# Where the seven-product trick is applied in three SwiGLUs of a one-core trunk: up projections in place of down projections

## The chip, the cores and the metric

The kernel runs on one core of a Trainium2 chip. The metric is the device time of one execution in microseconds; the time before is the median of three runs. One more execution was recorded by the hardware profiler; all views of the profile come from it.

## What is computed

A decoder trunk of two layers over 512 tokens of width 1024, in float32. Each layer adds half a SwiGLU, then a mixer (an mLSTM in the first layer, native sparse attention in the second), then half a SwiGLU. There are thus four SwiGLUs, ffn0 to ffn3, with 2816 hidden columns each:

```python
def rmsnorm(x, g):
    return x * lax.rsqrt(jnp.mean(x * x, axis=-1, keepdims=True) + EPS) * g

def swiglu(h, w_in, w_out):
    a, b = jnp.split(h @ w_in, 2, axis=-1)
    return (jax.nn.silu(a) * b) @ w_out

for layer in range(DEPTH):
    h = h + 0.5 * swiglu(rmsnorm(h, ffn_norm[layer, 0]), ffn_w_in[layer, 0], ffn_w_out[layer, 0])
    ...
    h = h + 0.5 * swiglu(rmsnorm(h, ffn_norm[layer, 1]), ffn_w_in[layer, 1], ffn_w_out[layer, 1])
```

The mLSTM's result is normed per head and multiplied by `sigmoid(og)` before its output projection.

## The kernel before

Everything is kept transposed: the stream is eight tiles `h[b]` of 128 features by 512 tokens. A weight block holds eight strips of 128x128. A SwiGLU has 22 blocks `a` (for the silu), 22 blocks `b` and, for the way down, eight output blocks.

**Precision.** Every float32 operand is split into a high and a low part (`split`: ScalarE copies to the high part, VectorE subtracts it for the low one). `mm3` (matmuls on line 215) makes a product of three matmuls, hi x hi, hi x lo and lo x hi. So an up block with 512 tokens is 8 strips x 3 = 24 matmuls of 512 columns, and blocks `a` and `b` together are 48. PSUM takes eight banks of 512 columns.

**Weights.** `weight` hands out weights in the order that a dry run has recorded, and loads two ahead: SP starts the DMA into `wraw` (two buffers), ScalarE makes `whi` and VectorE `wlo` (three buffers each). `plan` puts other steps into the same order.

**Seven products.** Two neighbouring output blocks and two halves of the inner dimension make a 2x2 matrix of weight quarters; the two token halves of 256 columns make the other side 2x2. With sums and differences ("forms") of quarters on both sides, seven products replace eight. In the kernel before this is done in ffn0, ffn1 and ffn3 (`SEVEN`) on the way down: `gate_forms` makes the forms of the gated tiles (`fhi`, `flo`), `fetch` loads four quarters, `add_quarters` makes four sums `s`, `load_forms` splits them in four groups, and `down_seven` runs the seven products of 256 columns into the banks X, Y, Z and V and combines them. The hidden blocks are taken in chunks of 8, 8 and 6 (`EVENS`); of each chunk's four pairs of output blocks, `PAIRS` picks two, two and one for seven products. That makes 15 such pairs in the kernel, twelve with 7 x 4 x 3 = 84 matmuls in place of 48, three with 63 in place of 36. All up blocks, the other down pairs and all of ffn2 are plain.

**Norm.** The up products run on `h` times the gain (`norm_in`: `xhi`, `xlo`). The row factor `r` comes later: `rstd_columns` and `rsqrt`, a chain of eleven small VectorE steps (`rq`, `rc`), then `rstd_rows`, whose matmul `cst,rc` spreads `rc`; the gates multiply by `r`. In ffn0 these are issued in up block 1, at its fourth and thirteenth strip. ffn1 and ffn3 get `r` from the stage before.

**Start.** `setup` loads `h[0]` to `h[7]`, the gains and the first two weights; up block 0 alternates strips of its two halves by a sort key.

**mLSTM.** In `finish` (lines 680 to 760) the numerators `num`, the denominators `ds`, `dc` and the head norm are made; `sigmoids(half)` (line 765) turns `og` into `sig` on ScalarE, and is issued before the `finish` of its half.

The engines run their own queues in order; a scheduler sets the order of one queue's instructions beforehand, from the order and the data needs of the program.

Of the kernel before, what the change touches and what calls it, by code (L numbers as in the profile page):

```python
# [10 lines left out]
F32 = mybir.dt.float32  # L11
# [8 lines left out]
P = 128  # L20
T = 512
# [8 lines left out]

SEVEN = (0, 1, 3)
EVENS = ((0, 8), (8, 16), (16, 22))
PAIRS = {0: (1, 3), 8: (1, 3), 16: (1,)}
# [63 lines left out]
class Net:  # L97
# [64 lines left out]
    def fetch(self, i, m, k0, n):  # L162


        q = {}
        for a in (1, 2):
            for b in (1, 2):
                k = k0 + (b - 1) * n
                t = q[a, b] = self.fp.tile([P, 512], F32, name=f"q{a}{b}", tag=f"q{a}{b}", bufs=1)[:, :n * P]
                ap = self.a["ffn_out"][i, 2 * m + a - 1, slice(None), slice(k, k + n)]  # L170
                self.nc.sync.dma_start(t.rearrange("p (n m) -> p n m", m=P), ap)
        self.raws[i, m, k0] = q

    def add_quarters(self, i, m, k0, n):

        q = self.raws[i, m, k0]
        s = self.sums[i, m, k0] = [None] + [self.fp.tile([P, 512], F32, name=f"s{j}", tag=f"s{j}", bufs=1)[:, :n * P]
                                            for j in range(1, 5)]
        self.nc.vector.tensor_tensor(s[1], q[2, 1], q[2, 2], op=ALU.add)
        self.nc.vector.tensor_tensor(s[3], q[1, 1], q[2, 1], op=ALU.subtract)  # L180
        self.nc.vector.tensor_tensor(s[2], s[1], q[1, 1], op=ALU.subtract)
        self.nc.vector.tensor_tensor(s[4], q[1, 2], s[2], op=ALU.subtract)

    def load_forms(self, i, m, k0, n, group):

        q, s = self.raws[i, m, k0], self.sums[i, m, k0]
        forms = ((q[1, 1], s[2]), (s[1], s[3]), (s[4], q[1, 2]), (q[2, 2],))[group]
        hi = self.wp.tile([P, 1024], F32R, name="whi", tag="whi")
        lo = self.wp.tile([P, 1024], F32R, name="wlo", tag="wlo")
        out = []  # L190
        for j, f in enumerate(forms):
            c = slice(512 * j, 512 * j + n * P)
# [35 lines left out]
    def setup(self):  # L228
# [7 lines left out]
        for b in range(KB):  # L236
# [5 lines left out]
            if b == 1 and self.order:  # L242
                self.load_weight()
# [11 lines left out]
    def norm_in(self, gcol, ssq=True, loaded=False):  # L255
# [82 lines left out]
    def ffn(self, i, r=None):  # L338
# [4 lines left out]
        with ExitStack() as ctx:  # L343
# [8 lines left out]
            def gated(t, pa, pb):  # L352
                u = gp.tile([P, T], F32, name="fu", tag="fu", bufs=2)
                TT(t, pa, r, op=ALU.mult)  # L354
                nc.scalar.activation(t, t, AF.Silu)
                TT(u, pb, r, op=ALU.mult)  # L356
                TT(t, t, u, op=ALU.mult)

            def gate(pa, pb):
                t = gp.tile([P, T], F32, name="ft", tag="ft", bufs=2)  # L360
                gated(t, pa, pb)
# [5 lines left out]
            def gate_forms(pa, pb):  # L367


                fl = lambda t: t.rearrange("p f n -> p (f n)")  # L370
                if not half:
                    t = gp.tile([P, 3 * N], F32, name="ft", tag="ft", bufs=2)
                    gated(t[:, :T], pa, pb)
                    TT(t[:, T:], t[:, :N], t[:, N:T], op=ALU.subtract)
                    hi = gp.tile([P, 8, N], F32R, name="fhi", tag="fhi", bufs=4)
                    lo = gp.tile([P, 8, N], F32R, name="flo", tag="flo", bufs=4)
                    self.split(t, fl(hi[:, :3]), fl(lo[:, :3]))
                    gs.append((hi, lo))
                    half.append(t)
                    return  # L380
                one, (hi, lo) = half.pop(), gs[-1]
                t = gp.tile([P, 5 * N], F32, name="fv", tag="fv", bufs=1)
                gated(t[:, :T], pa, pb)
                self.split(t[:, :T], fl(hi[:, 3:5]), fl(lo[:, 3:5]))
                c = [t[:, N * j:N * j + N] for j in range(5)]
                TT(c[2], c[0], one[:, T:], op=ALU.subtract)
                TT(c[3], c[0], one[:, :N], op=ALU.subtract)
                TT(c[4], c[1], c[2], op=ALU.subtract)  # L388
                self.split(t[:, T:], fl(hi[:, 5:]), fl(lo[:, 5:]))

            def down_plain(m, k0, n):

                w2 = [self.weight("ffn_out", i, 2 * m + j, slice(None), slice(k0, k0 + n)) for j in range(2)]
                if seven and m + 1 in PAIRS[k0]:
                    self.plan("fetch", i, m + 1, k0, n // 2)
                    self.plan("add", i, m + 1, k0, n // 2)
                po = [ps_mm() for _ in range(2)]
                order = [(k, j) for j in range(2) for k in range(n)]
                if m == 0:
                    order.sort(key=lambda o: (o[0] % (n // 2), o[0]) if seven else o)  # L400
                for k, j in order:
                    if seven:
                        f = slice(3 * (k // (n // 2)), 3 * (k // (n // 2)) + 2)
                        g = tuple(t[:, f, :].rearrange("p f n -> p (f n)") for t in gs[k % (n // 2)])
                    else:
                        g = gs[k]
                    first = order.index((k, j)) == min(order.index((q, j)) for q in range(n))
                    last = order.index((k, j)) == max(order.index((q, j)) for q in range(n))
                    self.mm3(po[j], self.strip(w2[j], k), g, first, last)
                    yield  # L410
                for j in range(2):
                    h = self.h[2 * m + j]
                    tail = i == 3 and k0 + n == FB and m == KB // 2 - 1 and j
                    for c in (slice(0, T // 2), slice(T // 2, T)) if tail else (slice(0, T),):
                        STT(h[:, c], po[j][:, c], 0.5, h[:, c], op0=ALU.mult, op1=ALU.add)  # L415

            def down_seven(m, k0, n):

                at = i, m, k0, n

                def product(ps, w, f):
                    for k in range(n):
                        l = w[0][:, k, :], w[1][:, k, :]
                        self.mm3(ps, l, (gs[k][0][:, f, :], gs[k][1][:, f, :]), k == 0, k == n - 1)
                        yield

                h1, h2 = self.h[2 * m], self.h[2 * m + 1]
                X, Y, Z, V = ps_mm(), ps_mm(), ps_mm(), ps_mm()
                two = lambda t: t.rearrange("p (c n) -> p c n", n=N)
                W = gp.tile([P, 3, N], F32, name="fw", tag="fw", bufs=2)  # L430
                u2 = gp.tile([P, N], F32, name="fq", tag="fq", bufs=1)
                q = gp.tile([P, T], F32, name="fr", tag="fr", bufs=1)
                a11, s2 = self.weight("form", *at, 0)
                yield from product(X[:, :N], a11, 1)
                nc.scalar.activation(W[:, 1, :], X[:, :N], AF.Copy)  # L435
                yield from product(X[:, N:], s2, 5)

                TT(u2, X[:, N:], W[:, 1, :], op=ALU.add)
                s1, s3 = self.weight("form", *at, 1)
                yield from product(Y[:, :N], s1, 2)  # L440
                yield from product(Y[:, N:], s3, 6)

                TT(W[:, 0::2, :], u2[:, None, :].to_broadcast([P, 2, N]), two(Y), op=ALU.add)
                TT(q[:, :N], W[:, 2, :], Y[:, :N], op=ALU.add)
                s4, a12 = self.weight("form", *at, 2)
                yield from product(Z[:, :N], s4, 3)
                yield from product(Z[:, N:], a12, 4)

                TT(W[:, :2, :], W[:, :2, :], two(Z), op=ALU.add)
                STT(h1, W[:, :2, :].rearrange("p c n -> p (c n)"), 0.5, h1, op0=ALU.mult, op1=ALU.add)  # L450
                a22 = self.weight("form", *at, 3)[0]
                yield from product(V[:, :N], a22, 7)

                TT(q[:, N:], W[:, 2, :], V[:, :N], op=ALU.add)
                STT(h2, q, 0.5, h2, op0=ALU.mult, op1=ALU.add)

            for k0, k1 in EVENS if seven else THIRDS:
                gs, late, half = [], [], []
                n = k1 - k0
                for p in range(k0, k1):  # L460
                    w2 = self.weight("ffn_in", i, p), self.weight("ffn_in", i, FB + p)
# [863 lines left out]
```

## Time and profile before

| | before |
|---|---|
| median of three runs (lowest, highest) | 2036.55 us (2036.38, 2037.76) |
| the profiled execution | 2037.12 us |
| its span, first to last instruction | 2035.3 us |
| GpSimd busy | 163.7 us (8%) |
| HBM read | 177.10 MB |
| moved by DMA, mean over the span | 92 GB/s |

Lines of the profile name the engine (PE is TensorE's matmuls, PEld its weight loads, DVE VectorE, ACT ScalarE), the line of the kernel and the tiles, result first. "x" is a count. In the groups, busy time and mean duration come first, then the idle time just before and who ended it. Matmuls overlap, so the time that one costs is read from start to start of its neighbours, not from its duration.

### The profile page before, as it was taken

What the parts mean: (1) busy time and instruction counts of PE and PEld (TensorE: products, weight loads), DVE (VectorE), ACT (ScalarE), POOL (GpSimd) and SP (SyncE); (2) the same over time, 40 slices, a digit from 0 to 9 for tenths busy, and PEclk for the clock granted to TensorE, in tenths of its full rate; (3) what the DMA queues carried; (4) which work ended last, traced back from release to release, by engine and by line L of the source; (5) the groups of instructions that cost most, each with busy time, mean ns of one, the idle gap of its engine ahead of it and who ended that gap; (6) DMA issues with size and microseconds to landing.
All of it is one profiled execution on the core that took longest, in us unless ns stands there. A gap on an engine that the chain in (4) does not pass through costs nothing.

```text
span 2035.3 us, 26085 instructions
## 1 busy us (share of the span) xinstructions
PE 2020.1 (99%) x10007; PEld 1677.1 (82%) x10007; DVE 1298.4 (64%) x2192; ACT 885.7 (44%) x1533; POOL 163.7 (8%) x216
## 2 busy tenths in 40 slices
PE   9999999999999999999999999999999999999999
PEld 7888888788778888888888888888777788888887
DVE  7565656767786655657656444445778885565654
ACT  5333334445743333334443322224889863333332
POOL 0000000012200000000101000001444410000000
PEclk9999999999999999999999999999999999999999
DMA  5333322323223333322333333323111123233232
GB/s 189 98 99 94 95 91 68 117 83 94 63 99 103 89 108 94 88 94 88 99 116 115 115 93 93 104 89 102 52 43 43 42 80 102 78 118 94 74 111 80
DMA packets 61084, 188.22 MB, mean 92 GB/s; under 512 B 7328, under 2 KB 9760, under 8 KB 60960
## 3 DMA queue, kind: packets, MB, share of 16 engines
q1 hardware_dynamic: 59568, 183.82, 29.3%
q8 instruction: 78, 1.28, 0.3%
q10 hardware_dynamic: 1008, 1.70, 0.2%
q0 software_dynamic: 384, 1.05, 0.2%
q14 instruction: 46, 0.38, 0.1%
HBM read 177.10 MB, written 2.10 MB: 88 GB/s over the span
## 4 chain that ended last, share of the span: by engine, by line
PE 92%; DVE 3%; ACT 3%; DMA 1%; issue 1%; POOL 0%; SPq 0%; DVEq 0%; ACTq 0%
PE pmm L215 82%; PE S L215 3%; PE po L215 2%; PE vps L215 1%; PE pt L1094 1%; PE paux L215 1%; ACT pr L1062 1%; PE pn L215 1%; DVE wlo L158 1%; ACT whi L157 0%; ACT pth L224 0%; PE pt L215 0%; PE dm L215 0%; DMA q<-in_ffn_out 0%; DMA wraw<-in_ffn_in 0%
## 5 line engine op out<-in xcount | busy, mean ns | idle before, releaser
L215 PE MATMUL pmm<-xhi,whi 128*128 128x512 f32 x1672 | 656.6, 393 | 0.7 <-ACT whi L157 0.5
L215 PE MATMUL pmm<-xhi,wlo 128*128 128x512 f32 x1672 | 652.8, 391 | 0.2
L215 PE MATMUL pmm<-xlo,whi 128*128 128x512 f32 x1672 | 652.3, 390 | 0.6 <-DVE xlo L268 0.6
L157 ACT ACTIVATE whi<-wraw 128x1024 fp32r<-128x1024 f32 (+5 forms) x368 | 329.7, 908 | 640.7 <-PE pmm L215 510.8
L158 DVE TENSOR_TENSOR wlo<-wraw,whi 128x1024 fp32r<-128x1024 f32 (+5 forms) x368 | 386.0, 1057 | 75.2 <-ACT whi L157 73.0
L215 PEld LDWEIGHTS pmm<-xhi,wlo 128*128 128x128 f32 x1672 | 313.4, 187 | 66.7 <-DVE wlo L158 1.1
L215 PEld LDWEIGHTS pmm<-xhi,whi 128*128 128x128 f32 x1672 | 313.7, 188 | 63.6 <-ACT whi L157 1.0
L215 PEld LDWEIGHTS pmm<-xlo,whi 128*128 128x128 f32 x1672 | 313.6, 188 | 62.7 <-DVE xlo L268 1.4
L215 PE MATMUL pmm<-fhi,whi 128*128 128x256 f32 (+1 forms) x699 | 230.9, 330 | 0.0
L215 PE MATMUL pmm<-flo,whi 128*128 128x256 f32 (+1 forms) x699 | 229.0, 329 | 0.0
L215 PE MATMUL pmm<-fhi,wlo 128*128 128x256 f32 (+1 forms) x699 | 228.8, 328 | 0.0
L356 DVE TENSOR_TENSOR fu<-pmm,r 128x512 f32<-128x512 f32 x88 | 60.8, 691 | 252.3 <-PE pmm L215 252.3
L215 PEld LDWEIGHTS pmm<-fhi,whi 128*128 128x128 f32 x699 | 132.7, 190 | 14.8 <-ACT fw L435 2.8
L215 PEld LDWEIGHTS pmm<-flo,whi 128*128 128x128 f32 x699 | 132.7, 190 | 11.9
L215 PEld LDWEIGHTS pmm<-fhi,wlo 128*128 128x128 f32 x699 | 132.6, 190 | 11.8
L415 DVE SCALAR_TENSOR_TENSOR h<-pmm,h 128x512 f32<-128x512 f32 (+1 forms) x67 | 45.5, 682 | 116.4 <-PE pmm L215 116.4
L278 POOL TENSOR_TENSOR ssq<-ssq,sq 128x512 f32<-128x512 f32 x18 | 26.5, 1470 | 1038.2 <-ACT sq L277 1006.0
L1067 POOL TENSOR_SCALAR pr<-pr,rz,gate 128x512 f32<-128x512 f32 (+3 forms) x128 | 81.8, 645 | 108.7 <-DVE rz L1063 92.9
L224 ACT ACTIVATE fhi<-fv 128x512 fp32r<-128x512 f32 x66 | 48.8, 740 | 84.2 <-DVE fv L388 61.0
L1062 ACT ACTIVATE pr<-S,nx,c 128x512 f32<-128x512 f32 (+3 forms) x128 | 78.1, 615 | 6.7 <-PE pt L1094 5.6
L354 DVE TENSOR_TENSOR ft<-pmm,r 128x512 f32<-128x512 f32 x55 | 37.9, 688 | 57.2 <-PE pmm L215 50.9
L224 ACT ACTIVATE whi<-s 128x512 fp32r<-128x512 f32 (+1 forms) x60 | 33.8, 601 | 89.9 <-PE pmm L215 63.7
(341 smaller groups left out, 2762.2 us busy)
## 6 DMA issues: line engine op xcount, KB each, us to landing
wraw<-in_ffn_in SPq DMA_DIRECT2D x175, 512.0 KB, 3.5
wraw<-in_ffn_out SPq DMA_DIRECT2D x32, 512.0 KB, 3.6
q<-in_ffn_out SPq DMA_DIRECT2D x48, 256.0 KB, 2.8
wraw<-in_ffn_out SPq DMA_DIRECT2D x16, 448.0 KB, 3.3
wraw<-in_ffn_out SPq DMA_DIRECT2D x18, 384.0 KB, 3.2
wraw<-in_m_qk SPq DMA_DIRECT2D x8, 512.0 KB, 3.5
wraw<-in_m_v SPq DMA_DIRECT2D x8, 512.0 KB, 3.6
wraw<-in_m_og SPq DMA_DIRECT2D x8, 512.0 KB, 3.5
```

The source lines that it names most:

```text
L157: nc.scalar.activation(hi[:p, c], raw[:p, c], AF.Copy)
L158: nc.vector.tensor_tensor(lo[:p, c], raw[:p, c], hi[:p, c].bitcast(F32), op=ALU.subtract)
L215: self.nc.tensor.matmul(out, lhsT, rhs, start=start, stop=stop)
L224: self.nc.scalar.activation(hi, src, AF.Copy)
L278: (nc.gpsimd if b < 4 else nc.vector).tensor_tensor(t, t, sq, op=ALU.add)
L354: TT(t, pa, r, op=ALU.mult)
L356: TT(u, pb, r, op=ALU.mult)
L415: STT(h[:, c], po[j][:, c], 0.5, h[:, c], op0=ALU.mult, op1=ALU.add)
L1062: nc.scalar.activation(s, S[:, i, :n], AF.Exp, bias=nx[:, i:i + 1], scale=cc, accum_out=z[:, i:i + 1])
L1067: nc.gpsimd.tensor_scalar(s, s, rz[:, i:i + 1], gate[:, tb, gi:gi + 1], op0=ALU.mult, op1=ALU.mult)
L1094: nc.tensor.transpose(pt[:, col:col + P], pr[br][:, ROW[tb] + sb * P:ROW[tb] + sb * P + P], self.ident)
```

## The change

The way down is plain again: `PAIRS`, `gate_forms` and `down_seven` go. In ffn0, ffn1 and ffn3 the up blocks are taken in pairs. The first pair (`p` = 0) stays plain. For each of the ten others the two `a` blocks are plain (2 x 24 matmuls of 512 columns), and the two `b` blocks are made by seven products (84 of 256 columns) instead of 48 of 512: `up_seven`. `fetch` takes quarters of `ffn_in`; `x_forms(k)`, four times per SwiGLU, makes four forms `thi`, `tlo` of 256 columns from `h[k]` and `h[k+4]`. Between the first product into X and the second one, a product into Y is issued.

Two smaller edits: at the start, the second weight is loaded after `h[3]` instead of `h[1]`, the rest of the first one is split one tile later, and the sort key of block 0 puts two more strips of the first half ahead of the second half's first strip. In the mLSTM, `sigmoids(half)` is issued inside `finish`, behind the Square that makes `dc`. Without the seven-product layout, the host no longer permutes `ffn_out`.

```diff
-PAIRS = {0: (1, 3), 8: (1, 3), 16: (1,)}
...
     def fetch(self, *at):
+        i, p = at
...
-                ap = self.a["ffn_out"][i, 2 * m + a - 1, slice(None), slice(k, k + n)]
+                ap = self.a["ffn_in"][i, FB + p + a - 1, slice(None), slice(4 * b - 4, 4 * b)]
...
     def load_forms(self, i, p, group):
-        forms = ((q[1, 1], s[2]), (s[1], s[3]), (s[4], q[1, 2]), (q[2, 2],))[group]
+        forms = ((q[1, 1], s[1]), (s[2], s[3]), (s[4], q[1, 2]), (q[2, 2],))[group]
...
-            if b == 1 and self.order:
+            if b == 3 and self.order:
                 self.load_weight()
...
-            if loaded and b == 1:
+            if loaded and b == 2:
                 self.rest()
...
+            def x_forms(k):
+                g1, g2 = (self.g[:, G_FFN + i * KB + b:G_FFN + i * KB + b + 1] for b in (k, k + 4))
+                one, two = (gp.tile([P, 3 * N], F32, name="fw", tag="fw", bufs=2) for _ in range(2))
+                h2, c = self.h[k + 4], [two[:, N * j:N * j + N] for j in range(3)]
+                nc.scalar.activation(one[:, :T], self.h[k], AF.Copy, scale=g1)
+                TT(one[:, T:], one[:, N:T], one[:, :N], op=ALU.subtract)
+                STT(c[0], h2[:, N:], g2, one[:, T:], op0=ALU.mult, op1=ALU.subtract)
+                STT(c[1], h2[:, N:], g2, one[:, N:T], op0=ALU.mult, op1=ALU.subtract)
+                STT(c[2], h2[:, :N], g2, c[0], op0=ALU.mult, op1=ALU.subtract)
+                hi = gp.tile([P, 4 * N], F32R, name="thi", tag="thi", bufs=4)
+                lo = gp.tile([P, 4 * N], F32R, name="tlo", tag="tlo", bufs=4)
+                self.split(one[:, T:], hi[:, :N], lo[:, :N])
+                self.split(two, hi[:, N:], lo[:, N:])
+                xt.append((hi, lo))
...
+            def up_seven(p):
...
+                a11, s1 = self.weight("form", i, p, 0)
+                yield from product(X[:, :N], a11, 0)
+                nc.scalar.activation(W[:, 0, :], X[:, :N], AF.Copy)
+                yield from product(Y[:, :N], s1, -1)
+                s2, s3 = self.weight("form", i, p, 1)
+                yield from product(X[:, N:], s2, -2)
+                TT(U, X[:, N:], W[:, 0, :], op=ALU.add)
+                yield from product(Y[:, N:], s3, -3)
+                TT(W[:, 1:, :], U[:, None, :].to_broadcast([P, 2, N]), two(Y), op=ALU.add)
+                TT(u2[:, N:], W[:, 2, :], Y[:, :N], op=ALU.add)
+                s4, a12 = self.weight("form", i, p, 2)
+                yield from product(Z[:, N:], s4, 3)
+                yield from product(Z[:, :N], a12, 2)
+                TT(two(u1), W[:, :2, :], two(Z), op=ALU.add)
+                TT(u1, u1, r, op=ALU.mult)
+                a22 = self.weight("form", i, p, 3)[0]
+                yield from product(V[:, :N], a22, -4)
+                TT(u2[:, :N], W[:, 2, :], V[:, :N], op=ALU.add)
+                TT(u2, u2, r, op=ALU.mult)
+                return u1, u2
...
+            def plain(p):
...
                 if p == 0:
-                    order.sort(key=lambda o: o[0] + 1.5 * o[1])
+                    order.sort(key=lambda o: o[0] + 3.5 * o[1])
...
+                    if seven and p == 1 and t >= 12:
+                        x_forms(t - 12)
...
+                    if seven and p:
+                        for j in range(2):
...
+                            if j == 0:
+                                self.plan("fetch", i, p)
+                            w = self.weight("ffn_in", i, p + j)
+                            if j == 0:
+                                self.plan("add", i, p)
+                            pa = ps_mm()
+                            for k in range(KB):
+                                strip(pa, w, k)
+                                yield
+                            ts.append(silu(pa))
+                        us = yield from up_seven(p)
+                        for t, u in zip(ts, us):
+                            gate(t, u)
...
                 nc.scalar.activation(dc, pt[:, :, :H], AF.Square)
+                sigmoids(half)
...
-            sigmoids(0)
             weave(project_v(1), finish(0), 0.25)
...
-            sigmoids(1)
             weave(finish(1), rest, 5)
```

How the order of the queues changes is shown at three places.

First, PE in ffn0, behind the first product of 256 columns into bank X. Before, row by row (line, operation, result<-operands, columns, what the instruction waits for; the number in a wait only names a semaphore):

```order
L215 MATMUL pmm<-fhi,whi 128x256
L215 MATMUL pmm<-flo,whi 128x256
L215 MATMUL pmm<-fhi,wlo 128x256
L215 MATMUL pmm<-fhi,whi 128x256 [waits Activation_49]
L215 MATMUL pmm<-flo,whi 128x256
L215 MATMUL pmm<-fhi,wlo 128x256 [waits DVE_49]
L215 MATMUL pmm<-fhi,whi 128x256
L215 MATMUL pmm<-fhi,whi 128x256 [waits Activation_49]
L215 MATMUL pmm<-flo,whi 128x256
L215 MATMUL pmm<-fhi,wlo 128x256
```

The new order, at the first `up_seven`, from the end of the product into Y on:

```order
L212 MATMUL pmm<-thi,whi 128x256
L212 MATMUL pmm<-tlo,whi 128x256
L212 MATMUL pmm<-thi,wlo 128x256
L212 MATMUL pmm<-thi,whi 128x256 [waits Activation_49]
L212 MATMUL pmm<-tlo,whi 128x256
L212 MATMUL pmm<-thi,wlo 128x256
L212 MATMUL pmm<-thi,whi 128x256 [waits Activation_49]
L212 MATMUL pmm<-tlo,whi 128x256
L212 MATMUL pmm<-thi,wlo 128x256 [waits DVE_49]
L212 MATMUL pmm<-thi,whi 128x256
```

Before, the second product into X begins at the second `waits Activation` (the copy of X's first half), with four matmuls of the product into Y pulled ahead of it. Now it begins at the second `waits Activation` too, but behind the whole of that product: the six rows ahead of it are the last of twelve.

Second, VectorE in up block 1 of ffn0, where the chain `rv`, `rq`, `rc` is worked off. Before:

```order
L158 TENSOR_TENSOR wlo<-wraw,whi 128x1024 [waits DMAHW3_49,Activation_49]
L299 TENSOR_SCALAR rq<-rv 128x4 [waits DVE_49]
L300 TENSOR_SCALAR rc<-rq 128x4 [waits DVE_49]
L302 TENSOR_TENSOR rq<-rc 128x4 [waits DVE_49]
L303 SCALAR_TENSOR_TENSOR rq<-rq,rv 128x4 [waits DVE_49]
L304 SCALAR_TENSOR_TENSOR rc<-rq,rc 128x4 [waits DVE_49]
L302 TENSOR_TENSOR rq<-rc 128x4 [waits DVE_49]
L303 SCALAR_TENSOR_TENSOR rq<-rq,rv 128x4 [waits DVE_49]
L304 SCALAR_TENSOR_TENSOR rc<-rq,rc 128x4 [waits DVE_49]
L302 TENSOR_TENSOR rq<-rc 128x4 [waits DVE_49]
L303 SCALAR_TENSOR_TENSOR rq<-rq,rv 128x4 [waits DVE_49]
```

Now, over the same start of the chain (`fw` and `tlo` are of `x_forms`):

```order
L296 TENSOR_SCALAR rq<-rv 128x4 [waits DVE_49]
L156 TENSOR_TENSOR wlo<-wraw,whi 128x1024 [waits DMAHW3_49,Activation_49]
L297 TENSOR_SCALAR rc<-rq 128x4 [waits DVE_49]
L377 TENSOR_TENSOR fw<-fw 128x256
L299 TENSOR_TENSOR rq<-rc 128x4 [waits DVE_49]
L379 SCALAR_TENSOR_TENSOR fw<-h_74,gains,fw 128x256
L300 SCALAR_TENSOR_TENSOR rq<-rq,rv 128x4 [waits DVE_49]
L378 SCALAR_TENSOR_TENSOR fw<-h_74,gains,fw 128x256
L301 SCALAR_TENSOR_TENSOR rc<-rq,rc 128x4 [waits DVE_49]
L222 TENSOR_TENSOR tlo<-fw,thi 128x256 [waits Activation_49]
L299 TENSOR_TENSOR rq<-rc 128x4 [waits DVE_49]
L380 SCALAR_TENSOR_TENSOR fw<-h_74,gains,fw 128x256
```

The small steps stood together and now alternate with those of `x_forms`; up to the last `rc` there are nine operations of `x_forms` and one more `wlo`. In PE's order, 27 strip matmuls stood between `ones,ssq` and `cst,rc`, and now 36.

Third, ScalarE at the end of the mLSTM's second half. Before:

```order
L224 ACTIVATE th<-sqn 128x512 [waits Activation_49]
L765 ACT_TABLE_LOAD
L765 ACTIVATE sig<-sig 128x512 x4
L708 COPY ds<-dm 40x512 [waits PE_49]
L157 ACTIVATE whi<-wraw 128x512 [waits DMAHW6_49,PE_49]
L157 ACTIVATE whi<-wraw 128x512
L714 ACTIVATE dc<-pnm 128x32 [waits PE_49]
```

Now:

```order
L221 ACTIVATE th<-sqn 128x512 [waits Activation_49]
L720 COPY ds<-dm 40x512 [waits PE_49]
L726 ACTIVATE dc<-pnm 128x32 [waits PE_49]
L779 ACT_TABLE_LOAD
L779 ACTIVATE sig<-sig 128x512 x4
L155 ACTIVATE whi<-wraw 128x512 [waits DMAHW0_49,PE_49]
L155 ACTIVATE whi<-wraw 128x512
```

The copy `ds` and the Square `dc` stood behind the table load and the sigmoids, and now stand ahead of them.

More of the change, by code (lines that the diff above doesn't have):

```diff
@@ L365, in gate @@
                 gs.append((hi, lo))
[L367 to L428, printed above, removed]
+            new_u = lambda: gp.tile([P, T], F32, name="fu", tag="fu", bufs=2)
@@ L429, in down_seven @@
+            def up_seven(p):
+                X, Y, Z, V = (ps_mm() for _ in range(4))
                 two = lambda t: t.rearrange("p (c n) -> p c n", n=N)
                 W = gp.tile([P, 3, N], F32, name="fw", tag="fw", bufs=2)
[L431 to L446, printed above, removed]
@@ new lines, in ffn @@
+            xt, columns, rows, late = [], [], [], []
+            for k0, k1 in EVENS if seven else THIRDS:
+                gs = []
+                for p in range(k0, k1, 2) if seven else range(k0, k1):
+                    if seven and p:
+                        ts = []
+                        for j in range(2):
[7 more added lines that the diff above has]
+                                strip(pa, w, k)
+                                yield
+                            ts.append(silu(pa))
+                        us = yield from up_seven(p)
+                        for t, u in zip(ts, us):
+                            gate(t, u)
+                        continue
+                    for j in range(2) if seven else range(1):
+                        yield from plain(p + j)
+                    if p or seven:
+                        if r is None:
+                            r = rows[0]
+                        while late:
+                            gate_plain(*late.pop(0))
+                n = k1 - k0
+                for m in range(0, KB, 2):
+                    w2 = [self.weight("ffn_out", i, m + j, slice(None), slice(k0, k1)) for j in range(2)]
+                    po = [ps_mm() for _ in range(2)]
+                    order = [(k, j) for j in range(2) for k in range(n)]
+                    if m == 0:
+                        order.sort()
+                    for k, j in order:
+                        self.mm3(po[j], self.strip(w2[j], k), gs[k], k == 0, k == n - 1)
+                        yield
+                    for j in range(2):
+                        h = self.h[m + j]
+                        last = i == 3 and k1 == FB and m + j == KB - 1
+                        for c in (slice(0, T // 2), slice(T // 2, T)) if last else (slice(0, T),):
+                            STT(h[:, c], po[j][:, c], 0.5, h[:, c], op0=ALU.mult, op1=ALU.add)
```

97 lines of the change are left out of this document (45 added, 52 removed).

## The prediction

> **What bounds the kernel now.** I began with the page's totals, its slices and its chain.
>
> ```profile
> span 2035.3 us, 26085 instructions
> PE 2020.1 (99%) x10007; PEld 1677.1 (82%) x10007; DVE 1298.4 (64%) x2192; ACT 885.7 (44%) x1533; POOL 163.7 (8%) x216
> PEclk9999999999999999999999999999999999999999
> PE 92%; DVE 3%; ACT 3%; DMA 1%; issue 1%; POOL 0%; SPq 0%; DVEq 0%; ACTq 0%
> ```
>
> TensorE has work in 99% of the span, at the full clock in every slice, and carries 92% of the chain. Since matmuls are pipelined, a busy PE could still run below its pace, so I next read the timeline of PE at the borders of four blocks of the first SwiGLU (start, duration, engine, line, operation, tiles).
>
> ```profile
> 97.35 0.39 PE L215 MATMUL pmm<-fhi,whi 128*128 128x512 f32 x1
> 108.23 0.28 PE L215 MATMUL pmm<-fhi,whi 128*128 128x256 f32 x1
> 118.55 0.40 PE L215 MATMUL pmm<-fhi,whi 128*128 128x512 f32 x1
> 139.78 0.40 PE L215 MATMUL pmm<-xhi,whi 128*128 128x512 f32 x1
> 226.85 0.39 PE L215 MATMUL pmm<-fhi,whi 128*128 128x512 f32 x1
> ```
>
> From 97.35 to 108.23 lies a plain down pair, 48 matmuls of 512 columns: 10.88 us. From 108.23 to 118.55 lies a pair by seven products, 84 matmuls of 256 columns: 10.32 us. From 139.78 to 226.85 lie eight plain up blocks, 384 matmuls: 87.07 us, 0.2267 us each, as in the down pair. So the pace doesn't drop; time goes where matmuls go, and at the few places where PE stands. The windows of three stretches (length, busy time of PE, PEld, DVE, ACT and POOL, clock, DMA share, GB/s) show what stands beside it.
>
> ```profile
> 97.35:108.23 10.88, 10.88 (x49) 9.01 (x48) 5.54 (x10) 3.28 (x6) 0.00 (x0) 1.00 0.10 26
> 108.23:118.55 10.32, 10.32 (x85) 10.11 (x84) 9.02 (x16) 4.68 (x7) 0.00 (x0) 1.00 0.26 62
> 145.00:225.00 80.00, 80.00 (x354) 66.25 (x353) 45.30 (x60) 28.30 (x33) 0.00 (x0) 1.00 0.32 100
> ```
>
> In plain stretches VectorE is busy 51 to 57%; in the pair by seven it is busy 87%, and the weight loads 98%.
>
> **The change, part by part: matmuls.** Inside the 10.32 us there is one stop, seen in the timelines of PE and ACT; the last line, from the view of line L435, says who waited for it over the span (us, times).
>
> ```profile
> 109.91 0.28 PE L215 MATMUL pmm<-fhi,wlo 128*128 128x256 f32 x1
> 110.03 0.66 PE L215 MATMUL pmm<-fhi,whi 128*128 128x256 f32 x2
> 110.52 0.28 PE L215 MATMUL pmm<-flo,whi 128*128 128x256 f32 x1
> ...
> 109.86 0.38 ACT L435 ACTIVATE fw<-pmm 128x256 f32<-128x256 f32 x1
> ...
>   PEld pmm L215: 2.8, 14
> ```
>
> Three starts (110.03, one inside the row of two, 110.52) take 0.49 us where two steps of 0.12 would take 0.24: 0.25 us are lost while ScalarE copies the first half of bank X, before PE may write the second half. Without it the 84 matmuls take 10.07 us, 0.120 each. The copy runs 15 times (its row is below), and 14 times the loads of PE waited for it, so I count the stop in all 15 pairs. In the changed order twelve matmuls into bank Y stand between the product that the copy reads and the next write to X: 12 x 0.12 = 1.44 us of cover for a 0.38 us copy that starts once its product has ended. I count the stop as gone.
>
> New: 30 up pairs (ten in each of three SwiGLUs) go from 10.88 to 10.07 us: -0.81 x 30 = -24.3. Taken back: 12 down pairs of eight strips rise from 10.32 to 10.88, +0.56 x 12 = +6.7; three of six strips rise from 63 x 0.12 + 0.25 = 7.81 to 36 x 0.2267 = 8.16, +0.35 x 3 = +1.1. **Matmuls: -16.5 us.** If every new pair kept the stop, it would be 30 x 0.25 = 7.5 less: -9.0.
>
> A rule speaks on the pace. The Trainium skill ("TensorE: Matmul & The Clock Gate", § Back-to-back issue gap) gives N/2.4 + 2.5 ns for a single matmul's gap, 215.8 ns at 512 columns and 109.2 ns at 256. With 756 fewer matmuls of 512 and 1323 more of 256 columns, an estimate by it is -163.1 + 144.4 = -18.7, against -171.4 + 158.8 = -12.6 by this trace's two paces, both without the stops; by the trace, small matmuls cost slightly more than half of large ones, and the trace decides.
>
> **VectorE beside it.** Its work for one up pair, by the groups of instructions (columns: count | busy us, mean ns | idle before):
>
> ```profile
> L158 DVE TENSOR_TENSOR wlo<-wraw,whi 128x1024 fp32r<-128x1024 f32 x223 | 274.4, 1231 | 39.0 <-ACT whi L157 38.5
> L225 DVE TENSOR_TENSOR wlo<-s,whi 128x512 fp32r<-128x512 f32 x48 | 31.9, 686 | 0.2
> L179 DVE TENSOR_TENSOR s<-q,q 128x512 f32<-128x512 f32 x12 | 8.7, 725 | 0.0
> L438 DVE TENSOR_TENSOR fq<-pmm,fw 128x256 f32<-128x256 f32 x15 | 6.4, 425 | 11.6 <-PE pmm L215 11.3
> L356 DVE TENSOR_TENSOR fu<-pmm,r 128x512 f32<-128x512 f32 x88 | 60.8, 691 | 252.3 <-PE pmm L215 252.3
> L435 ACT ACTIVATE fw<-pmm 128x256 f32<-128x256 f32 x15 | 5.7, 381 | 2.8 <-PE pmm L215 2.3
> ```
>
> Two plain weights 2 x 1.231 = 2.46; seven forms 7 x 0.686 = 4.80; four sums 4 x 0.725 = 2.90; three combinations of 256 columns 1.28 and four operations of 512 on them 2.76; for the two gates six operations of 0.69, 4.14. That is 18.3 us against a PE period of 10.88 + 10.07 = 20.95: 88%, as in the pair by seven of before, where nothing but the copy stopped PE. I cost it at nothing; PE's own 20.95 us hides it, and the cover ends if VectorE's work and waits pass that. ScalarE's share is smaller in every stretch. The bytes loaded don't change: quarters of 256 KB replace raw weights of 512 KB, on the same queue. Where the last up pair runs into the down projection, its gates end later than those of a plain block; for nine such places I add +0.5 (0 to +3), worked from one 256-column combination and two operations of 0.69 that stand behind the last matmul and that the down order by strips lets PE reach last.
>
> **First pair.** `x_forms` runs four times beside up block 1.
>
> ```profile
> 23.14 0.16 DVE L311 TENSOR_SCALAR rv<-pmm 128x4 f32<-128x4 f32 x1
> 23.26 0.69 DVE L182 TENSOR_TENSOR s<-q,s 128x512 f32<-128x512 f32 x1
> ...
> 26.79 0.16 DVE L303 SCALAR_TENSOR_TENSOR rq<-rq,rv 128x4 f32<-128x4 f32 x1
> 26.99 0.16 DVE L304 SCALAR_TENSOR_TENSOR rc<-rq,rc 128x4 f32<-128x4 f32 x1
> 28.43 1.05 PE L215 MATMUL pmm<-cst,rc 128*128 128x128 f32 x8
> ...
> L225 DVE TENSOR_TENSOR flo<-fv,fhi 128x768 fp32r<-128x768 f32 x33 | 31.6, 958 | 27.4 <-ACT fhi L224 27.4
> L386 DVE TENSOR_TENSOR fv<-fv,ft 128x256 f32<-128x256 f32 x33 | 13.8, 419 | 0.0
> ```
>
> In ffn0 its operations enter VectorE's queue between the small steps of the rsqrt, whose last result `rc` came at 27.15. Ahead of it there now stand eight more of 256 columns (8 x 0.42), one of 768 (0.96) and one weight (1.23): 5.5 us of work by durations. A small step needs 0.12 us before the next, independent instruction starts (23.14 to 23.26), but 0.20 where the next waits for it (26.79 to 26.99), so the new work hides some 0.08 us of each of eleven, and larger instructions follow each other a little faster than their durations: 4.1 to 5.5. So `rc` comes at 31.3 to 32.7. PE has nine matmuls more ahead of the one that reads `rc`, so it gets there at 28.43 + 9 x 0.2267 = 30.47. It waits 0.8 to 2.2 us: **+1.5**, range 0 (if the scheduler's other operations slip behind) to +4 (if the forms of the first pair are late too). In ffn1 and ffn3 `r` exists already and no row of PE waits behind VectorE there: 0.
>
> **Start.** The window of the first loads, for PE alone (length, busy, clock, DMA share, GB/s):
>
> ```profile
> 5.70:10.60 4.90, 3.58 (x10) 1.00 1.01 386
> ```
>
> The DMA engines are full there; the first strips come at the pace of landings. The second weight now loads after h3 rather than h1, so the second half's strips start later and the first half's earlier; the bytes that must land before the 48th matmul are the same: **+0.3** (-0.5 to +1).
>
> **Sigmoids.** At the end of the mLSTM's second half, ScalarE and PE:
>
> ```profile
> 554.84 1.28 ACT L765 ACT_TABLE_LOAD   x1
> 556.13 2.19 ACT L765 ACTIVATE sig<-sig 128x512 f32<-128x512 f32 x4
> 558.23 0.56 ACT L708 COPY ds<-dm 40x512 f32<-40x512 f32 x1
> ...
> 555.60 0.50 PE L215 MATMUL dm<-tl,hot 128*128 128x512 f32 x1
> ...
> 572.00:581.00 9.00, 7.86 (x28) 4.69 (x28) 7.89 (x15) 3.98 (x8) 0.00 (x0) 1.00 0.21 71
> ```
>
> `ds` needs only `dm`, done about 556.1, and waits to 558.23 behind table and sigmoids: 2.1 us. The denominators behind it start that much earlier. The cost of before shows at 572 to 581, where 28 matmuls take 9.0 us instead of 28 x 0.2267 = 6.35, 2.65 lost. I take **-2.0**, between -3 and +0.5: not all of it, since VectorE is busy 7.89 of those 9 us, and the sigmoids now stand ahead of later work on ScalarE.
>
> **Sum.** -16.5 - 2.0 + 1.5 + 0.3 + 0.5 = -16.2, so 2035.3 becomes 2019.1. The profiled execution took 2037.12, 1.8 more than its span; the median of the runs, 2036.55, lies 0.6 under it. 2036.55 - 16.2 = 2020.35; I say **2020.5**.
>
> **The rivals.**
> *A small stop stays in every new pair* (the copy still late, or a form or its sum a little behind). For it: 98% busy loads and 87% busy VectorE leave PE no spare, and one stop of 0.25 us did sit in each of 15 pairs. Against it: the only one seen has a named cause that the new order removes. 30 x 0.25 = 7.5: 2028.
>
> *The forms of x stall the first pair of all three SwiGLUs*, 3 us each instead of 1.5 in one: +7.5, also 2028. Against it: up block 1 is followed by 10.88 us of gate matmuls before a form is needed, about the 12 us that they cost VectorE.
>
> *VectorE's queue sets the up pair* (the other side). It works in order; a combination that waits for a product stops the weights and forms queued behind it, which the next products need. 18.3 us of work plus more than 2.65 us of such waits pass PE's period, and beyond 20.95 + 16.2/30 = 21.5 us the kernel is slower than before. With 4 us of waits: 22.3, 30 x 1.35 = +40, 2061. Against it: `wlo<-s` waited 0.2 us in 48 cases, and the combinations wait at places where PE itself is the late one.
>
> *A page's rule: loads.* In this trace a small matmul's weight load is as long as its data, 10.11 us in 10.32. If loads could not hide in the new place, each of 1323 matmuls would cost a load of 10.11/84 = 0.12, what it costs already; if PE ever paid the two in series, 0.24 each, +159, about 2180. The Trainium skill ("Perfetto Trace Analysis", § Identifying the Most-Contended Engine) says to judge TensorE by the busy share of its weight loads. By that rule this change, with 567 more loads, raises the busiest resource. The trace of the 84 matmuls speaks against a loss: they run at 0.120 with all their loads.
>
> *Sigmoids change nothing*: +2, inside my range.
>
> **How the numbers follow.** My forecast (2015 to 2025) has 0.68; a stop in each pair or stalled first pairs (2025 to 2032) 0.21; a gain of less than 4 us for several of these together 0.04; VectorE's queue 0.06; serial loads 0.01. What a measurement can tell from no change is about 0.2%, 4 us. The bounds of the separate costs added up give -16.5 to -9.0 for matmuls, -3 to +0.5, 0 to +4, -0.5 to +1, 0 to +3: 2016.5 to 2036; since they won't all end on one side I stop at 2031; below I go to 2015, past the sum of the low ends, for waits of the old gates that the trace doesn't separate. Faster 0.89, same 0.04, slower 0.07.
>
> **What would show it.** Up pairs of the changed kernel should repeat every 21.0 us: 48 matmuls of 512 columns in 10.88, 84 of 256 in 10.07, and no wait of PE for the copy of X. 20.95 right but more time elsewhere: look at 28 to 33 us for `rc`, and at the nine entries to a down projection. A period of 21.2 is the first rival; one over 21.5, with PE waiting for `wlo`, the third. `ds` should follow `dm` at once, and the stretch of 28 matmuls should shrink by 2 us. Most doubtful are VectorE's 88% and ffn0's first pair.

## The result and the profile after

| | before | changed |
|---|---|---|
| median (lowest, highest) | 2036.47 us (2036.38, 2037.76) | 2024.55 us (2024.05, 2025.58) |
| ratio, 95% interval | | 0.9941 (0.9923 to 0.9958) |
| profiled execution; its span | 2037.12; 2035.3 us | 2025.58; 2023.8 us |

The kernel is 11.9 us faster. The forecast was 16, so about three quarters of it came. The page of the changed kernel (span; busy time and instructions; shares of the chain that ended last):

```profile
span 2023.8 us, 27493 instructions
PE 2007.7 (99%) x10574; PEld 1695.5 (84%) x10574; DVE 1342.6 (66%) x2309; ACT 900.7 (45%) x1626; POOL 164.5 (8%) x216
PE 88%; DVE 6%; ACT 4%; issue 1%; DMA 1%; POOL 0%; SPq 0%; DVEq 0%; ACTq 0%; POOLq 0%
```

PE has 567 instructions more and 12 us less to do. Its share of the chain fell from 92 to 88%, VectorE's rose from 3 to 6%. So there are new places where PE waits, and the next step is to find them, stage by stage: not in the pairs, whose borders stand in PE's timeline like this:

```profile
141.16 0.39 PE L212 MATMUL pmm<-xhi,whi 128*128 128x512 f32 x1
...
152.04 0.28 PE L212 MATMUL pmm<-xhi,whi 128*128 128x256 f32 x1
...
161.99 0.28 PE L212 MATMUL pmm<-thi,wlo 128*128 128x256 f32 x1
```

48 matmuls of 512 columns take 152.04 - 141.16 = 10.88 us; the 84th small one starts at 161.99, one step of 0.12 before 162.11: 10.07 us. Both are the forecast's figures. The starts of the small products follow at 20.98 us from pair to pair in each of the three SwiGLUs, where 20.95 had been forecast; only ffn0's first new pair takes 21.67. (The 0.03 lies in the `a` blocks: behind a run of small matmuls the first large ones start a little further apart, and the 48 take 10.91 us.) VectorE does not fill them (windows; length, busy PE, PEld, DVE, ACT, POOL, clock, DMA share, GB/s):

```profile
162.10:183.10 21.00, 21.00 (x135) 19.11 (x134) 16.54 (x28) 8.72 (x14) 0.00 (x0) 1.00 0.34 105
```

16.5 of 21.0 us: 79% rather than the forecast's 88%. The sum of durations (18.3) counted overlapping ends of neighbouring instructions twice: at 97.44 and 98.04 us, for one, two start 0.60 us apart, and the first is 0.69 long.

Three places did lose time. The sums of the norm (`ones,ssq`), which stand behind 57 strip matmuls, began at 22.94 instead of 21.36 (the first row is of the kernel before, the others of the changed one). In ffn3 PE waits for `rc`. And in one stretch of the attention stage the clock fell:

```profile
21.36 0.39 PE L215 MATMUL pmm<-ones,ssq 128*128 128x1 f32 x3
...
22.94 0.28 PE L212 MATMUL pmm<-ones,ssq 128*128 128x1 f32 x2
...
1686.67 0.60 PE L212 MATMUL pmm<-cst,rc 128*128 128x128 f32 x3 [1.16 <-DVE rc L301]
...
1515.00:1516.00 1.00, 1.00 (x8) 0.73 0.00 0
1516.00:1517.00 1.00, 1.00 (x8) 0.50 0.00 0
1517.00:1518.00 1.00, 1.00 (x5) 0.50 0.00 0
1518.00:1519.00 1.00, 1.00 (x5) 0.56 0.00 0
```

The last rows (length, PE busy, clock, DMA share, GB/s) show half the clock for some 3.4 us with PE working throughout, which costs 1.7. Of the twelve other kept traces only that of `pad4` shows one there. The two executions of the changed kernel with a mean clock of 1.000 took 2024.05 and 2024.06, and one of the six of `both2`, at a mean clock of 0.79, took 3658.9 us and is left out of its time below. Single executions thus differ by one or two microseconds, and effects of that size are read below from the stages in the traces, not from medians.

The mLSTM (from the first matmul into `pg` to the last on `yhi`, `ylo`) took 366.9 to 597.9 before and takes 364.3 to 593.3 now, 2.0 less, as forecast.

### The profile page after: what moved, and what is told of

Its sections match the earlier page's. It is cut to its first block, busy times and chain, and to the rows that moved or that the text cites. A ratio compares the mean times of both kernels' runs of the same rounds, so it can differ in the third digit from the quotient of the medians.

```text
span 2023.8 us, 27493 instructions
## 1 busy us (share of the span) xinstructions
PE 2007.7 (99%) x10574; PEld 1695.5 (84%) x10574; DVE 1342.6 (66%) x2309; ACT 900.7 (45%) x1626; POOL 164.5 (8%) x216
## 4 chain that ended last, share of the span: by engine, by line
PE 88%; DVE 6%; ACT 4%; issue 1%; DMA 1%; POOL 0%; SPq 0%; DVEq 0%; ACTq 0%; POOLq 0%
PE pmm L212 78%; PE S L212 3%; PE po L212 2%; PE vps L212 1%; PE pt L1106 1%; ACT pr L1074 1%; PE paux L212 1%; DVE wlo L156 1%; PE pn L212 1%; DVE xlo L265 1%; ACT whi L155 0%; DVE tlo L222 0%; ACT pth L221 0%; PE dm L212 0%; ACT nx L1071 0%
## 5 line engine op out<-in xcount | busy, mean ns | idle before, releaser
L212 PE MATMUL pmm<-xhi,whi 128*128 128x512 f32 (+1 forms) x1552 | 571.8, 368 | 0.6 <-ACT whi L155 0.4
L212 PE MATMUL pmm<-xhi,wlo 128*128 128x512 f32 (+1 forms) x1552 | 568.1, 366 | 0.7 <-DVE wlo L156 0.4
L212 PE MATMUL pmm<-xlo,whi 128*128 128x512 f32 (+1 forms) x1552 | 567.8, 366 | 0.5 <-DVE xlo L265 0.5
L212 PE MATMUL pmm<-ghi,whi 128*128 128x512 f32 x704 | 274.2, 390 | 0.0
L212 PE MATMUL pmm<-glo,whi 128*128 128x512 f32 x704 | 274.0, 389 | 0.0
L212 PE MATMUL pmm<-ghi,wlo 128*128 128x512 f32 x704 | 273.6, 390 | 0.0
L212 PEld LDWEIGHTS pmm<-ghi,wlo 128*128 128x128 f32 x704 | 132.2, 188 | 28.9 <-DVE wlo L156 1.6
L212 PE MATMUL pmm<-thi,wlo 128*128 128x256 f32 x480 | 135.9, 283 | 0.0
L212 PE MATMUL pmm<-thi,whi 128*128 128x256 f32 x480 | 135.8, 283 | 0.0
L212 PE MATMUL pmm<-tlo,whi 128*128 128x256 f32 x480 | 135.8, 283 | 0.0
```

What stands on the lines that cost most here:

```text
L212: self.nc.tensor.matmul(out, lhsT, rhs, start=start, stop=stop)
```

## The experiments

Eleven kernels. Theory A is a ledger: the pairs give what was forecast, and the missing time lies at single places. Theory B spreads it over the pairs, or finds another cause for the same rows.

**start_old.** The start as before, the rest as changed.

```diff
-            if b == 3 and self.order:
+            if b == 1 and self.order:
...
-            if loaded and b == 2:
+            if loaded and b == 1:
...
-                    order.sort(key=lambda o: o[0] + 3.5 * o[1])
+                    order.sort(key=lambda o: o[0] + 1.5 * o[1])
```

> The changed kernel with the start as before: second weight after h1, rest of the first one a tile earlier, sort key 1.5. Theory A (the new pairs give what was forecast, and what is missing lies at single places, the start among them: the 57 strip matmuls ahead of the norm's sums end at 22.7 us now and ended at 21.1 before): they end near 21.1 again, the span is 1.5 us shorter, about 2022.5. Theory B (the start only looks late because the small matmuls ahead of the first strip ran at half pace for longer in the profiled execution, and what is missing is spread over the pairs): no change, 2024, with those 57 matmuls ending near 21.1 in both orders whenever the early matmuls reach full pace at 4 us.

Measured: 2025.73 us (ratio to before 0.9945, 0.9931 to 0.9960). The timelines of PE and VectorE, and windows of PE:

```profile
21.41 0.28 PE L212 MATMUL pmm<-ones,ssq 128*128 128x1 f32 x2
...
1681.92 0.39 PE L212 MATMUL pmm<-xhi,wlo 128*128 128x512 f32 x1
1685.36 2.08 PE L212 MATMUL pmm<-cst,rc 128*128 128x128 f32 x8 [3.04 <-DVE rc L301]
...
1683.70 0.16 DVE L299 TENSOR_TENSOR rq<-rc 128x4 f32<-128x4 f32 x1
1683.81 1.23 DVE L156 TENSOR_TENSOR wlo<-wraw,whi 128x1024 fp32r<-128x1024 f32 x1
1684.95 0.15 DVE L300 SCALAR_TENSOR_TENSOR rq<-rq,rv 128x4 f32<-128x4 f32 x1
...
1682.00:1684.00 2.00, 0.31 (x2) 1.00 0.58 225
1684.00:1686.00 2.00, 0.64 (x3) 0.76 0.02 4
1686.00:1688.00 2.00, 2.00 (x9) 0.50 0.91 262
```

The start gains 22.94 - 21.41 = 1.5 us, as A said. B is out: here too the early matmuls ran at half pace until 5.7 us, and in `sig_early`, with the new start, they were fast from 4.1 us on and the sums still began at 22.74. The three edits were undone together; which of them costs what is not shown. But the time didn't fall: in ffn3 the scheduler now put a weight's split between the small steps of the rsqrt, PE stood for 3.04 us instead of 1.16, and then ran at half the clock for some 3 us. A miss in the total, with its cause in sight.

**forms_rc.** In ffn3, the gains for two of the four `x_forms` are copied by a step that reads `rc`, so that they queue behind it.

```diff
+                if i == 3 and k >= 2:
+                    if k == 2:
+                        gg.append(gp.tile([P, KB], F32, name="gg", tag="gg", bufs=1))
+                        STT(gg[0], columns[0][:, :1].to_broadcast([P, KB]), 0.0, self.g[:, G_FFN + i * KB:G_FFN + i * KB + KB], op0=ALU.mult, op1=ALU.add)
+                    g1, g2 = gg[0][:, k:k + 1], gg[0][:, k + 4:k + 5]
...
```

> The changed kernel, with the forms of h2/h6 and h3/h7 in ffn3 made to depend on rc (their gain is copied through a small step that reads rc), so that they stand behind the rsqrt chain in VectorE's queue. Theory A: the 1.3 us for which PE waits for rc at 1686 us goes, and nothing else is late since a form is first needed some 16 us later: 1.0 to 1.3 us shorter, about 2022.9. Theory B: the wait comes back as a wait for a late form in ffn3's first new pair, and the time stays at 2024.

Measured: 2025.74 us (0.9948, 0.9932 to 0.9965); the total is B's, but not its reason. PE no longer waits for `rc` (the row of `cst,rc` at 1683.55 names no wait), and no form is late. Instead the plain down projections of ffn3 start a matmul every 0.2337 us on average, instead of 0.2275. The next two kernels take this apart.

**shift32.** Only the 32-byte tile.

```diff
+                if i == 3 and k == 2:
+                    nc.vector.memset(gp.tile([P, KB], F32, name="gg", tag="gg", bufs=1)[:, :1], 0.0)
```

> The changed kernel with only the 32-byte tile of forms_rc in ffn3 (one small memset writes a column of it, nothing reads it). Theory A (the shifted place of the gate tiles in memory sets the pace of the matmuls that stream them): ffn3's plain down projections run at 0.2335 us a matmul instead of 0.2267, 3.3 us longer there. Theory B (the moved VectorE work of forms_rc did it): 0.2267 as in the changed kernel.

Measured: one time, 2026.89 us. The wait for `rc` is back (1.2 us). The first matmul of ffn3's first down projection and the first one behind it, in this kernel and then in the changed one:

```profile
1751.27 0.40 PE L212 MATMUL pmm<-ghi,whi 128*128 128x512 f32 x1
1796.15 0.39 PE L212 MATMUL pmm<-xhi,whi 128*128 128x512 f32 x1
...
1753.35 0.40 PE L212 MATMUL pmm<-ghi,whi 128*128 128x512 f32 x1
1797.03 0.39 PE L212 MATMUL pmm<-xhi,whi 128*128 128x512 f32 x1
```

The 192 matmuls take 44.88 us, 0.2337 each, against 43.68, 0.2275 each. ffn0 and ffn1 keep 0.2275, and the pairs of ffn3, which don't read the gated tiles, keep 20.98. So the shifted place of the tiles does it.

**rc_home.** `forms_rc` with the copied gains in unused columns of a small tile that exists.

```diff
-            nc.vector.memset(gp.tile([P, 96], F32, name="home", tag="home", bufs=1)[:, :1], 0.0)
+            home = gp.tile([P, 96], F32, name="home", tag="home", bufs=1)
+            nc.vector.memset(home[:, :1], 0.0)
...
+                if (i, k) in ((3, 2), (3, 3)):
+                    if not late_gain:
+                        late_gain.append(home[:, 64:64 + KB])
+                        STT(late_gain[0], columns[0][:, :1].to_broadcast([P, KB]), 0.0, self.g[:, G_FFN + i * KB:G_FFN + i * KB + KB], op0=ALU.mult, op1=ALU.add)
+                    g1, g2 = late_gain[0][:, k:k + 1], late_gain[0][:, k + 4:k + 5]
...
```

> As forms_rc, but the copied gains lie in columns of an existing small tile, so that no tile of ffn3 moves. Theory A: forms_rc did remove the 1.3 us wait for rc, and gave it back because its new 32-byte tile shifted the tiles behind it, whose matmuls in the plain down projections then started every 0.2335 instead of 0.2267 us; with nothing moved the pace is 0.2267 again, the wait is gone, and the time is 1.3 us under the changed kernel's: about 2022.7. Theory B: the slower pace comes from the moved VectorE work; then the down projections of ffn3 stay at 0.2335 and the time at 2025.

Measured: 2022.34 us (0.9928, 0.9916 to 0.9940). The pace is 0.2275 again, and the wait is gone:

```profile
1682.93 1.05 PE L212 MATMUL pmm<-cst,rc 128*128 128x128 f32 x8
```

A holds, with 2.2 us under the changed kernel's median where 1.3 had been expected, and 1.7 under its executions at a mean clock of 1.000; ffn3 alone, from its sums to its last matmul, is 341.7 - 340.3 = 1.4 shorter.

**both2.** `rc_home` with the old start.

> rc_home and start_old together. Theory A: the two add, 1.4 for the start and 1.3 for rc, about 2021.3; the wait of nearly 3 us for rc that start_old had in ffn3, and the half clock after it, don't come. Theory B: the order of ffn3 shifts once more and a wait for rc or for a form stays; 2022.5 or more.

Measured: 2021.33 us (0.9927, 0.9914 to 0.9939). The sums begin at 21.36, ffn3 has neither wait nor slow clock: A. The gain over `rc_home` is 1.0 and not 1.4, as in ffn0 PE now gets to `rc` too early (a wait of 0.20 at 31.05): of the 1.3 us by which the sums begin sooner, 0.9 are left behind `rc`.

**sig_early.** The sigmoids back ahead of `finish`.

```diff
-                sigmoids(half)
...
+            sigmoids(0)
             weave(project_v(1), finish(0), 0.25)
...
+            sigmoids(1)
             weave(finish(1), rest, 5)
```

> The changed kernel with the sigmoids of both mLSTM halves ahead of finish, as before. Theory A: the copy ds stands behind table load and sigmoids again and the mLSTM is 2.0 us longer: about 2026. Theory B (PE has other work there, and the shorter mLSTM stage of the changed kernel comes from the order of its neighbours): within 0.5 us of 2024.

Measured: 2025.36 us (0.9944, 0.9929 to 0.9959). ScalarE in the changed kernel, then in this one:

```profile
553.70 0.58 ACT L720 COPY ds<-dm 40x512 f32<-40x512 f32 x1 [1.31 <-PE dm L212]
555.22 1.28 ACT L779 ACT_TABLE_LOAD   x1
556.51 2.19 ACT L779 ACTIVATE sig<-sig 128x512 f32<-128x512 f32 x4
```

```profile
552.03 1.28 ACT L778 ACT_TABLE_LOAD   x1
553.32 2.19 ACT L778 ACTIVATE sig<-sig 128x512 f32<-128x512 f32 x4
555.42 0.56 ACT L720 COPY ds<-dm 40x512 f32<-40x512 f32 x1
```

In front of the sigmoids `ds` runs as soon as PE has made `dm`; behind them it is 1.7 us later. The mLSTM stage takes 594.95 - 364.13 = 230.8 us instead of 229.0: 1.9 longer by the unrounded times, A. The medians differ by only 0.8; against the changed kernel's executions at a mean clock of 1.000 it is 1.3.

**x_direct.** The old order of products around bank X.

```diff
-        forms = ((q[1, 1], s[1]), (s[2], s[3]), (s[4], q[1, 2]), (q[2, 2],))[group]
+        forms = ((q[1, 1], s[2]), (s[1], s[3]), (s[4], q[1, 2]), (q[2, 2],))[group]
...
-                a11, s1 = self.weight("form", i, p, 0)
+                a11, s2 = self.weight("form", i, p, 0)
...
-                yield from product(Y[:, :N], s1, -1)
-                s2, s3 = self.weight("form", i, p, 1)
                 yield from product(X[:, N:], s2, -2)
                 TT(U, X[:, N:], W[:, 0, :], op=ALU.add)
+                s1, s3 = self.weight("form", i, p, 1)
+                yield from product(Y[:, :N], s1, -1)
```

> The changed kernel with the products of up_seven in the old order: the second product into bank X right behind the first (forms q11 and s2 in one weight, s1 and s3 in the next). Theory A: each of the 30 pairs stops for the copy of X as the 15 down pairs of before did: 30 x 0.25 = 7.5 us longer, about 2031.5, with PE's loads waiting for the copy in 30 places. Theory B: the scheduler pulls other matmuls forward and hides the copy; under 2 us longer.

Measured: 2031.02 us (0.9973, 0.9962 to 0.9983), 6.5 longer, and 7.0 against the changed kernel's executions at a mean clock of 1.000: A. The view of the copy's line says who waited for it:

```profile
who waited for it (us, times):
  PEld pmm L212: 6.4, 30
```

The pairs follow at 21.23 instead of 20.98: the stop of 0.25 us, in all 30. For the same line the changed kernel lists nobody. The PSUM page of the Trainium skill ("PSUM — Partial Sum Buffer", § PSUM bank collisions raise a hardware error) gives a reason why PE is made to wait although the two halves of the bank are disjoint: two engines must not access one bank on the same partitions at once, whatever the columns, so software makes them take turns. The 30 waits agree; no run here let them overlap.

**pad4, pad8.** Four and eight additions on VectorE in each pair that nobody reads: `pad(1)`, or `pad(2)`, at four places.

```diff
+            def pad(n):
+                for _ in range(n):
+                    z = gp.tile([P, T], F32, name="pad", tag="pad", bufs=1)
+                    TT(z, self.h[0], self.h[1], op=ALU.add)
...
                 a11, s1 = self.weight("form", i, p, 0)
+                pad(1)
...
```

> The changed kernel with four idle additions of 512 columns on VectorE in each of the 30 new pairs, whose results nobody reads (output unchanged). It tells how near VectorE is to setting the pair. Theory A (its queue is bound by the starts, 0.60 us apart for such an operation: 15.9 us of the pair's 20.95 are taken): four more make 18.3, no change, within 3 us of 2024. Theory B (bound by durations: 18.3 of 20.95 are taken): four of 0.69 make 21.1, the pair takes 21.1 to 21.5, 5 to 16 us longer.

> As pad4 with eight such additions in each pair. Theory A (starts): 15.9 + 4.8 = 20.7, just under PE's 20.95; waits in the queue begin to show, 0 to 15 us longer. Theory B (durations): 18.3 + 5.5 = 23.8, 30 x 2.85 = 85 us longer, about 2110.

Measured: 2029.85 (0.9970) and 2029.44 us (0.9962), pairs at 20.98 in both. As a dose these two failed: needing nothing of the pair, the additions were mostly scheduled outside it, around the first pair and beside the down projections. There they showed something else: VectorE's queue counts ahead of `rc`. PE stands 1.8 us for it in ffn1 and 3.2 in ffn3 in both kernels. The sums of ffn0 begin 1.3 later; there PE also waits for a split weight, and the clock is at half for 3.4 us from 12.7 and 13.0 us on. Twice the additions cost no more, so the load isn't what costs, but the few of them that stand in front of a chain.

**padin6, padin12.** Six and twelve, in place on the `b` tiles ahead of the gate, so that they must run within a pair.

```diff
+                for u in (u1, u2):
+                    for _ in range(3):
+                        TT(u, u, u, op=ALU.max)
```

> The changed kernel with six more operations of 512 columns on VectorE in each new pair, in place on the two b tiles ahead of the gate (the larger of a value and itself: output unchanged), so that they can't leave the pair as those of pad4 and pad8 did. In the steady pairs of the changed kernel VectorE is busy 16.5 of 21.0 us. Theory A (VectorE isn't near to setting the pair; only a period above PE's counts): 16.5 + 6 x 0.6 to 0.69 = 20.1 to 20.6, pairs stay at 20.98 us; only the ends of the three runs of pairs before a down projection are later, 9 x up to 4 us, so up to some 20 us longer in all. Theory B (in-order waits take what is left): pairs of 22 us or more, over 30 us longer.

> As padin6, with twelve. Both theories: 16.5 + 12 x 0.6 to 0.69 = 23.7 to 24.8 us of work, so the pair is VectorE's: 2.7 to 3.8 us longer each, 30 x that = 80 to 115 us, plus the later ends; about 2110 to 2160. If pairs stay at 21, the busy time misleads and the work is smaller than it looks.

Measured: 2026.68 us (0.9952, 0.9933 to 0.9972) and 2099.81 us (1.031, 1.028 to 1.034). Windows of the steady pairs, the first four with six, then three with twelve:

```profile
141.00:225.00 84.00, 84.00 (x531) 76.41 (x530) 71.20 (x115) 34.63 (x54) 0.00 (x0) 1.00 0.27 87
...
170.48:239.31 68.83, 65.76 (x398) 57.84 (x397) 68.52 (x114) 26.70 (x42) 0.00 (x0) 1.00 0.28 91
```

With six the pairs stay at 20.98 us; in the last down projection of each of the three SwiGLUs PE loses 0.66 us in two waits, for a gated tile and for a split weight, and the SwiGLUs show no other stop that the changed kernel doesn't have. With twelve VectorE is busy 68.52 of 68.83 us, the three pairs take 22.9 us each on average, and 75 us are lost, some 5 less than A's and B's common estimate. So VectorE's queue can set the pair, but it takes more than six added operations.

## Why the prediction was right, and where it was off

The time lay in the range, close to its middle, 4 us above the forecast. By the forecast's own steps:

- **Matmuls, -16.5: right in mechanism, mis-sized by 1.7** (0.5 of it stood in the sum as late entries to the down projections). In ffn1 the way from the sums to the last matmul shrinks from 345.3 to 340.3 us, by 5.0 where a third of 16.5 is 5.5. By count and the trace's two paces each SwiGLU loses 4.2 us, 12.6 in all, as forecast. The estimate by the formula of the Trainium skill ("TensorE: Matmul & The Clock Gate", § Back-to-back issue gap) was 18.7, further off. The stops that went were 1.2, 1.2 and 0.95 us per SwiGLU, 3.3 where I had put 3.7. Some 1.1 us came back, most of it at the entries to the down projections, seen here in ffn0:

```profile
98.04 1.22 DVE L156 TENSOR_TENSOR wlo<-wraw,whi 128x1024 fp32r<-128x1024 f32 x1
...
99.09 0.72 PE L212 MATMUL pmm<-ghi,wlo 128*128 128x512 f32 x2
99.65 0.39 PE L212 MATMUL pmm<-ghi,whi 128*128 128x512 f32 x1
```

  The second of the two matmuls at 99.09 starts 0.33 us after the first, not 0.23: the split of the second weight ended only at 99.26. So stands the entry to the first two down projections of each SwiGLU; what is late is a weight, and not the gates that I had thought of. Behind its first twenty or so matmuls a down projection runs at the forecast's 0.2267 us; the 0.2275 above is the average with the entry.
- **The copy of X is covered: right**, by `x_direct` to the hundredth of a microsecond.
- **VectorE costs nothing in the pairs: right**, with more room than I had put (`padin6`). The weight loads, whose busy share rose from 82 to 84%, cost nothing either: the rival by the rule of the Trainium skill ("Perfetto Trace Analysis", § Identifying the Most-Contended Engine) is out.
- **First pair, +1.5 in ffn0 and 0 in ffn1 and ffn3: near in size, at 2.3, and wrong in place.** "In ffn1 and ffn3 `r` exists already" was wrong: the timeline of before has the sums and `cst,rc` in both, in ffn1 here:

```profile
610.99 0.39 PE L215 MATMUL pmm<-ones,ssq 128*128 128x1 f32 x3
...
618.07 0.61 PE L215 MATMUL pmm<-cst,rc 128*128 128x128 f32 x4
```

  In ffn3 the forms in VectorE's queue stopped PE for 1.2 us, 1.4 with the restart, as `rc_home` shows. In ffn0 the later start left almost nothing of the wait for `rc` (0.1 us; with the old start 0.6, in `both2`), but a first product waited 0.5 us for a split weight at 45.5 us, a term that I hadn't counted; all in all ffn0 lost 0.9. In ffn1 PE did not wait, though forms stand between the small steps there too. That the sum came near the forecast is chance.
- **Start, +0.3: mis-sized; it is 1.3 to 1.6** (`both2` against `rc_home`, `start_old`). I argued from bytes. By the traces, what counts is how much work PE has while strips land: with one weight it ran out after twelve matmuls and stood until the second one, landed at 9.2 instead of 7.9 us, was split; and the low parts of the later strips were queued behind that split on VectorE.
- **Sigmoids, -2.0: right** (2.0 by the stage, 1.9 by undoing it).
- **Between span and median.** Of the 16.2 forecast, the spans show 2035.3 - 2023.8 = 11.5, and 13.2 without the slow clock. The start (1.3), the matmuls (1.2 net of the late entries) and the first pairs (0.8) make 3.3; other stages gave 0.3 back. The medians differ by 11.9 because the profiled execution of before lay 0.65 above its median, and slow stretches hold the changed kernel's median 0.5 above its fastest.

## What to carry to other kernels

Count what a trick does to the bound engine at its measured pace: this held to 0.03 us in every pair but ffn0's first. The rest was decided at the seams, where a few small instructions of a chain (`rc`) share an in-order queue with new bulk work; hold the bulk back by a data dependence, and watch that the cure moves no tile. When a bank is read by one engine and written by another, put a product into another bank in between.

## What I had not expected of the hardware

- A 32-byte shift of the tiles that PE streams made each of its matmuls of 512 columns 2.7% slower (0.2337 for 0.2275 us, `shift32`, `forms_rc`).
- In every kept trace the clock changes only at whole steps of 3.413 us after it first came to full, and what counts is how a stop lies against these steps. Windows of PE by such steps (length, PE busy, clock, DMA share, GB/s), around the stop for `rc` in ffn3, in `start_old`, `pad8` and `pad4`:

```profile
1681.63:1685.05 3.42, 0.68 (x4) 1.00 0.39 143
1685.05:1688.46 3.41, 3.10 (x11) 0.50 0.56 161
...
1688.96:1692.37 3.41, 1.08 (x9) 1.00 0.53 159
1692.37:1695.79 3.42, 3.42 (x10) 0.50 0.23 75
...
1688.65:1692.07 3.42, 1.85 (x9) 1.00 0.08 10
1692.07:1695.48 3.41, 1.78 (x12) 1.00 0.41 149
1695.48:1698.90 3.42, 3.42 (x17) 1.00 0.22 77
```

  PE stood for 3.04 us in the first and for 3.19 in the other two. Where one step was idle for 2.7 or 2.3 us, the next ran at half clock; in `pad4` the stop lay across two steps, 1.6 us in each, and the clock stayed. The Trainium skill ("TensorE: Matmul & The Clock Gate", § What's actually happening) puts an idle window of about 3.4 us there; here 2.3 us of such a step were enough.
- The clock also fell without such a pause, in the attention stage of the changed kernel and of `pad4`. Both times the step ahead held the same 21 matmuls, 15 of them of 32 columns, with PE busy 3.12 of 3.41 us; in the eleven other traces the steps cut that stretch at other places, and the clock held. Why it fell there no run shows.
- The matmuls ahead of the first strip came to full pace at 4.0 us in one execution, 5.7 in another and 6.8 in a third. The sums of the norm showed little of it: 21.36 and 21.41 in the first two, which have the old start, and 22.94 in the third, against 22.45 to 22.84 in seven other kernels with the new start, fast between 4.1 and 5.9 us.
